# Layer 0's queries and keys projected by token instead of by feature, and the attention sink as a column of layer 1's scores

## Chip, core and metric

The kernel runs on one core of a Trainium2 chip. The metric is the device time of one execution in microseconds (us), lower is better; several runs are timed and their median counts. The engines are TensorE (PE; its weight loads are PEld), VectorE (DVE), ScalarE (ACT), GpSimd (POOL) and SyncE (SP), which here issues nearly all transfers.

## What is computed

A decoder trunk with two layers over 256 tokens of width 1024, all in float32. Layer 0 is causal attention over 16 heads of 64 (with 256 tokens its blocks of 256 leave plain causal attention), layer 1 is sliding-window attention (window 128) of 16 query heads over 4 shared key/value heads with a learned sink per head. Each layer ends in a gated FFN (width 2816) with a causal depthwise convolution of width 3. In each head the first 16 of 64 dimensions of queries and keys are rotated.

```python
def partial_rope(x, cos, sin):
    x1, x2 = x[..., :half], x[..., half:ROT_DIM]           # half = 8
    return concat([x1 * cos - x2 * sin, x2 * cos + x1 * sin, x[..., ROT_DIM:]])

# layer 0
h = rmsnorm(x, attn_norm[0])
q, k, v = split(h @ w_qkv_a[0], 3)
q, k = partial_rope(heads(q)), partial_rope(heads(k))
o = causal_attention(q, k, heads(v))
# layer 1
logits = where(band, q @ k.T / 8, NEG)
m = maximum(max(logits), sink)
e = exp(logits - m)
p = e / (sum(e) + exp(sink - m))
# both layers
x = x + o @ w_o
x = x + conv_ffn(rmsnorm(x, ffn_norm[l]), ...)
```

## The kernel before

**Precision and weights.** Every matmul is done in three: each operand is split into a high part (rounded to the fast float32 format of TensorE) and a low part, and high x high, high x low and low x high are added in PSUM. Weights come in 90 units of 128 x 2048 numbers (1 MB each, tile `wr`, three buffers). For each unit ScalarE makes the high part `wh` (`hi_part`, L173) and VectorE the low part `wl` (`lo_part`, L181), in two to eight pieces, four buffers each. Unit i + 3 is fetched when unit i has been split, and unit i + 4 is split when the matmuls of unit i have been issued. Units 2 to 7 and 10 to 11 are layer 0's query and key weights (two for each group of four heads), 0, 1, 8 and 9 its value weights, 12 to 15 its output weights.

**Order.** All engines' queues are filled by one Python program. It keeps a clock of estimated TensorE time (`tick`); work on other engines is put off with `chain(key, (delay, step), ...)` and issued when that clock has passed its time, or earlier when `require(key)` asks for it. So the delays in the code set the order in each engine's queue, and the queues are executed strictly in that order.

**Layer 0's queries and keys** (`qk_group`, `proj_f`, `rotate_f`). Weights are the stationary operand and the normalized activations the moving one (256 tokens), so the product has features on partitions and tokens in columns: one PSUM bank (`acc`, 128 x 512) holds two chunks of 128 features of q, another of k. Rotation in that layout: VectorE swaps neighbours within 32 partitions (`stream_shuffle`, L460), multiplies the bank and the swapped copy by two tables (L461, L462) and adds (L463); ScalarE makes the high part (L466), VectorE the low part (L471). The tables `tab` have cosines and sines by feature and token, already multiplied by the token's 1/rms; `new_tables` scales them by token on ScalarE (L433) and turns them with four transposes on TensorE (L440). Group 0 is projected with its q and k banks in turn, groups 1 to 3 one bank after the other.

**Layer 1's queries and keys** (`proj`, `rotate`, `rope`, `to_feature`) already go by token: activations stationary, weights moving, the product scaled by 1/rms as ScalarE copies it out of PSUM (L1098), rotated on VectorE in four small operations on the 16 rotated dimensions (L391, L396 twice, L397), transposed by TensorE (L403), split into high (ScalarE, L414) and low part (VectorE, L409).

**Attention.** For each of four groups: `scores` (18 matmuls), for each head a mask and a running minimum on VectorE (`masked`, L548), exponentials with their sum on ScalarE (`exps`, L558), reciprocal and scaling (`norm`, VectorE L569 and L576, ScalarE L574), transposes of the probabilities on TensorE (`probs_T`, L589) with copies out of PSUM (L595, L597), and `values` (L612). Between these, `fill` puts matmuls of a filler: projections of the next groups and of the other half of v (L362 to L364), then the output projection (L662 to L667). `spread` copies the first token block of k into a block-diagonal tile `kd` on GpSimd (L1002), which the scores of the first token block need. Of PSUM there are four banks `acc`, two `u` and two `t`.

**The sink** in layer 1: the minimum of negated scores starts at -sink (`nsink`), a ScalarE exponential gives exp(sink - m) for each head (L561), and VectorE adds it to the sum (L567).

Of the kernel before, what the change touches and what calls it, by code (L numbers as in the profile page):

```python
# [7 lines left out]
F32 = mybir.dt.float32  # L8
# [52 lines left out]
def trunk(ctx: ExitStack, tc, x, xw, pos, cpk, fin, sinks, w, out):  # L61
# [26 lines left out]
    def row3(n=3 * P):  # L88
        return wk.tile([P, 3 * P], F32, tag="m3", name=nm("m3"), bufs=8)[:, :n]
# [308 lines left out]

    def to_feature(t, n, b, hi, lo, key, then=None):

        pt = bank("t")
        for j in range(n):
            nc.tensor.transpose(pt[:, j * P:(j + 1) * P], t[:, j * P:(j + 1) * P], ident)  # L403
        tick(110 * n)
        v = pt[:, :n * P].rearrange("p (j t) -> p j t", j=n)
        hb, lb = hi[:, :, blk(b)], lo[:, :, blk(b)]

        def low():
            nc.vector.tensor_tensor(out=lb, in0=v, in1=f(hb), op=ALU.subtract)  # L409
# [12 lines left out]

    tab = [None]
    TURN = 7700.0

    def new_tables(rs_, key, between):

        ex = tab[0]
        sc = mid().rearrange("p (b k f) -> p b k f", b=NB, k=2)
        new = quad(F32, "tab")[:, :2]  # L430

        for b in range(NB):
            nc.scalar.activation(sc[:, b], ex[:, b].rearrange("p k e d -> p k (e d)"), AF.Copy, scale=rs_[b])  # L433
            between(b)

        def turn():
            t = bank("t")
            for b in range(NB):
                for k in range(2):
                    nc.tensor.transpose(t[:, k * S + b * P:k * S + (b + 1) * P], sc[:, b, k], ident)  # L440
            tick(440)
            chain(key, (300.0, lambda: copy(t)))

        def copy(t):
            nc.scalar.activation(new, t.rearrange("p (k t) -> p k t", k=2), AF.Copy)
            tab[0] = new

        chain(key, (TURN, turn))

    SWAP = [(i + HALF) % ROT if i < ROT else i for i in range(32)]  # L450

    def rotate_f(o, hi, lo, key, tkey, then=None):

        t, u = mid(), mid()
        t3, u3, o3 = (a.rearrange("p (c t) -> p c t", c=2) for a in (t, u, o))

        def turn():
            require(*tkey)
            c_, s_ = (tab[0][:, k].unsqueeze(1).to_broadcast([P, 2, S]) for k in range(2))
            nc.vector.stream_shuffle(u, o, SWAP)  # L460
            nc.vector.tensor_tensor(out=t3, in0=o3, in1=c_, op=ALU.mult)  # L461
            nc.vector.tensor_tensor(out=u3, in0=u3, in1=s_, op=ALU.mult)  # L462
            nc.vector.tensor_tensor(out=t, in0=t, in1=u, op=ALU.add)  # L463

        def high():
            nc.scalar.activation(hi, t3, AF.Copy)  # L466
            if then is not None:
                then(hi, 0)

        def low():  # L470
            nc.vector.tensor_tensor(out=lo, in0=t3, in1=f(hi), op=ALU.subtract)  # L471
            if then is not None:
                then(lo, 1)

        chain(key, (150.0, turn), (2600.0, high), (700.0, low))

    def proj_f(o, hT, wv, units=()):

        for m in range(2):
            om = o[:, m * S:(m + 1) * S]  # L480
            for c in range(KC):
                for b in range(NB):
                    require("x", b, c // 4)
                xh, xl = hx(hT, c)
                wh, wl = wv(c, m)
                nc.tensor.matmul(om, wh, xh, start=(c == 0), stop=False)
                nc.tensor.matmul(om, wh, xl, start=False, stop=False)
                nc.tensor.matmul(om, wl, xh, start=False, stop=(c == KC - 1))
                tick(3 * S / 2.4)
                if m and units and (c + 1) * len(units) % KC == 0:  # L490
                    used(units[(c + 1) * len(units) // KC - 1])
                yield 3 * S / 2.4

    def cols128(u, n_u, at):

        def wv(c, m):
            i, r = divmod(c * n_u, KC)
            need(u + i)
            w_ = UNIT * n_u // KC
            s_ = slice(r // n_u * w_ + at + m * P, r // n_u * w_ + at + (m + 1) * P)  # L500
            return tuple(t[:, s_] for t in wq[u + i])
        return wv

    def attention(qk, ready, filler, lead, rate, msk, vcol, sink):
# [35 lines left out]
        def softmax(j, p, sd, sab):  # L540
            pr = [row3() for _ in range(2)]
# [11 lines left out]
            def exps(e):  # L553
                h = 2 * j + e
                c2 = slice(2 * e, 2 * e + 2)
                for qb in range(NB):
                    c = slice(P, 3 * P) if qb else slice(0, P)
                    nc.scalar.activation(pr[e][:, c], pr[e][:, c], AF.Exp, scale=-1.0, bias=st[:, 0, 2 * e + qb:2 * e + qb + 1],  # L558
                                         accum_out=st[:, 1, 2 * e + qb:2 * e + qb + 1])
                if sink:  # L560
                    nc.scalar.activation(st[:, 2, c2], st[:, 0, c2], AF.Exp, bias=sink_t[:, h:h + 1])  # L561

            def norm(e):
                c2 = slice(2 * e, 2 * e + 2)
                total = st[:, 1, c2]
                if sink:
                    nc.vector.tensor_tensor(out=st[:, 2, c2], in0=total, in1=st[:, 2, c2], op=ALU.add)  # L567
                    total = st[:, 2, c2]
                nc.vector.reciprocal(st[:, 3, c2], total)  # L569
                for qb in range(NB):  # L570
                    c = slice(P, 3 * P) if qb else slice(0, P)
                    r = st[:, 3, 2 * e + qb:2 * e + qb + 1]
                    if qb:
                        nc.scalar.activation(pr[e][:, c], pr[e][:, c], AF.Copy, scale=r)  # L574
                    else:
                        nc.vector.tensor_scalar(out=pr[e][:, c], in0=pr[e][:, c], scalar1=r, scalar2=None, op0=ALU.mult)  # L576
# [371 lines left out]
    def tables():  # L948
        nc.vector.scalar_tensor_tensor(out=kk, in0=arg[:, 0], scalar=-1.0, in1=arg[:, 0], op0=ALU.mult, op1=ALU.max)
        nc.gpsimd.tensor_scalar(out=arg[:, 1], in0=kk, scalar1=-1.0, scalar2=HALF_PI, op0=ALU.mult, op1=ALU.add)  # L950
# [6 lines left out]
        ex = mid().rearrange("p (b k e d) -> p b k e d", b=NB, k=2, e=2)  # L957
        nc.gpsimd.memset(ex[:, :, 0, :, ROT:], 1.0)
        nc.gpsimd.memset(ex[:, :, 1, :, ROT:], 0.0)
        for k, t in enumerate((cs, sn)):  # L960
            for e in range(2):
                nc.gpsimd.tensor_copy(ex[:, :, k, e, :ROT], t)
        tab[0] = ex
# [48 lines left out]
    nc.gpsimd.tensor_scalar(out=nsink, in0=sink_t, scalar1=-1.0, scalar2=0.0, op0=ALU.mult, op1=ALU.add)  # L1012
# [43 lines left out]
    attention(qk, ready_a, filler_a(), 9000.0, lambda g: (7000.0, 3500.0, 2000.0) if g < 3 else (4500.0, 2000.0, 1500.0), mask, lambda h: h, False)  # L1056
# [12 lines left out]
    o_down[0].finish(3, after_a, by_half=True)  # L1069
    xT_h = new_hT()  # L1070
# [114 lines left out]
def pack(inp):  # L1185
# [14 lines left out]
    qk = [np.concatenate([q[:, :, g * 256:(g + 1) * 256], k[:, :, g * 256:(g + 1) * 256]], axis=2) for g in range(4)]  # L1200
# [72 lines left out]
```

## Time and profile before

| | |
|---|---|
| median of 3 runs | 558.45 us (557.94 to 558.82) |
| profiled execution | 559.24 us, span 557.2 us |
| granted TensorE clock | 0.999 |
| busy, share of span | PE 97%, PEld 91%, DVE 78%, ACT 68%, POOL 21% |
| HBM read | 99.30 MB, mean 180 GB/s |
| layer 0's attention | 16 to 118 us; layer 1's: 295 to 371 us |

The span is the time from the first to the last instruction of the profiled execution; the rest of its time lies around it. Busy time of TensorE counts matmuls whose ends are modelled and which overlap, so the distances between starts tell more than the shares. A group of instructions is told as line, engine, operation, out<-in, shapes, count, then busy us and mean ns of one, then the idle time before it and what ended it.

### The profile page before, as it was taken

The numbers are of one execution on the slowest core, as the hardware profiler recorded it, in microseconds if no ns is written. First come the engines' busy times: TensorE is split into PE (matmuls) and PEld (weight loads), VectorE is DVE, ScalarE is ACT, GpSimd is POOL, SyncE is SP. The second block draws the span as 40 slices with busy tenths as digits, with TensorE's granted clock in tenths as the row PEclk, the third lists the DMA queues.
The fourth block names the chain that finished last, engine by engine and source line by source line (L and its number), as shares of the span: only waits on it lengthen the run. The fifth ranks groups of instructions, "written<-read, shape, count | busy, mean of one in ns | idle before, by whom it ended". The sixth has DMA issues, their size and how long they took to land.

```text
span 557.2 us, 10523 instructions
## 1 busy us (share of the span) xinstructions
PE 543.3 (97%) x4022; PEld 507.3 (91%) x4022; DVE 435.8 (78%) x930; ACT 376.7 (68%) x765; POOL 115.1 (21%) x130
## 2 busy tenths in 40 slices
PE   9998999999999999999999999999999999999995
PEld 8997789889999999988888988889999999998884
DVE  6799888599888888873468988888888888884514
ACT  6749697779567777654358998887757777663313
POOL 8322202012333322210001000001632322210003
PEclk9999999999999999999999999999999999999999
DMA  8954462523365656666552724242375556666301
GB/s 326 372 204 168 155 228 92 212 80 149 131 248 205 199 207 223 226 227 203 184 216 89 289 78 151 76 145 85 123 256 191 203 213 226 233 228 215 118 0 75
DMA packets 15312, 101.00 MB, mean 181 GB/s; under 512 B 1952, under 2 KB 2080, under 8 KB 3744
## 3 DMA queue, kind: packets, MB, share of 16 engines
q1 hardware_dynamic: 14976, 100.09, 50.3%
q8 instruction: 31, 0.51, 0.4%
q10 hardware_dynamic: 288, 0.26, 0.1%
q14 instruction: 17, 0.14, 0.1%
HBM read 99.30 MB, written 1.05 MB: 180 GB/s over the span
## 4 chain that ended last, share of the span: by engine, by line
PE 76%; DVE 10%; ACT 5%; DMA 5%; issue 2%; POOL 0%; SPq 0%; DVEq 0%; POOLq 0%; ACTq 0%
PE acc L662 9%; PE acc L663 9%; PE acc L667 9%; PE u L758 6%; PE u L757 6%; PE u L759 6%; PE t L758 6%; PE t L757 6%; PE t L759 6%; DMA wr<-in_w 4%; DVE wl L181 3%; PE acc L757 2%; PE acc L759 2%; PE acc L758 2%; PE t L612 2%
## 5 line engine op out<-in xcount | busy, mean ns | idle before, releaser
L181 DVE TENSOR_TENSOR wl<-wr,wh 128x1024 fp32r<-128x1024 f32 (+1 forms) x190 | 208.1, 1111 | 49.5 <-ACT wh L173 49.2
L173 ACT ACTIVATE wh<-wr 128x1024 fp32r<-128x1024 f32 (+1 forms) x186 | 174.4, 964 | 52.0 <-PE acc L667 42.3
L803 POOL TENSOR_TENSOR m<-m,m 128x256 f32<-128x256 f32 x44 | 72.7, 1653 | 164.8 <-DVE m L798 99.3
L662 PE MATMUL acc<-wh,q 128*128 128x512 f32 x238 | 92.1, 387 | 0.0
L663 PE MATMUL acc<-wl,q 128*128 128x512 f32 x238 | 90.6, 380 | 0.0
L757 PE MATMUL u<-q,wh 128*128 128x256 f32 x320 | 88.3, 277 | 0.0
L758 PE MATMUL u<-q,wh 128*128 128x256 f32 x320 | 88.1, 276 | 0.0
L759 PE MATMUL u<-q,wl 128*128 128x256 f32 x320 | 87.9, 275 | 0.0
L757 PE MATMUL t<-q,wh 128*128 128x256 f32 x288 | 79.2, 275 | 0.0
L758 PE MATMUL t<-q,wh 128*128 128x256 f32 x288 | 79.2, 275 | 0.0
L759 PE MATMUL t<-q,wl 128*128 128x256 f32 x288 | 79.2, 275 | 0.0
L667 PE MATMUL acc<-wh,q 128*128 128x512 f32 x238 | 74.6, 379 | 0.0
L759 PEld LDWEIGHTS u<-q,wl 128*128 128x128 f32 x320 | 61.4, 192 | 0.0
L758 PEld LDWEIGHTS u<-q,wh 128*128 128x128 f32 x320 | 61.4, 192 | 0.0
L757 PEld LDWEIGHTS u<-q,wh 128*128 128x128 f32 x320 | 61.3, 192 | 0.0
L757 PEld LDWEIGHTS t<-q,wh 128*128 128x128 f32 x288 | 55.3, 192 | 0.0
L758 PEld LDWEIGHTS t<-q,wh 128*128 128x128 f32 x288 | 55.3, 192 | 0.0
L759 PEld LDWEIGHTS t<-q,wl 128*128 128x128 f32 x288 | 55.3, 192 | 0.0
L662 PEld LDWEIGHTS acc<-wh,q 128*128 128x128 f32 x238 | 45.0, 189 | 7.0 <-issue 0.7
L667 PEld LDWEIGHTS acc<-wh,q 128*128 128x128 f32 x238 | 45.0, 189 | 6.3
L663 PEld LDWEIGHTS acc<-wl,q 128*128 128x128 f32 x238 | 45.0, 189 | 5.9 <-issue 0.2
L807 ACT ACTIVATE q<-m 128x256 fp32r<-128x256 f32 x44 | 18.2, 416 | 45.4 <-POOL m L803 45.3
(191 smaller groups left out, 1152.6 us busy)
## 6 DMA issues: line engine op xcount, KB each, us to landing
wr<-in_w SPq DMA_DIRECT2D x90, 1024.0 KB, 4.8
first<-in_xw SPq DMA_DIRECT2D x5, 384.0 KB, 5.2
xr<-in_x SPq DMA_DIRECT2D x2, 512.0 KB, 8.4
first<-in_xw SPq DMA_DIRECT2D x1, 768.0 KB, 6.6
fin_t<-in_fin SPq DMA_DIRECT2D x1, 512.0 KB, 5.6
out<-ot SPq DMA_DIRECT2D x1, 512.0 KB, 2.6
first<-in_xw SPq DMA_DIRECT2D x1, 388.0 KB, 3.3
out<-m ACTq DMA_DIRECT2D x1, 256.0 KB, 2.1
```

Source lines behind the costliest of these rows:

```text
L173: nc.scalar.activation(wq[i][0][:, c], raws[i][:, c], AF.Copy, **({} if g is None else {"scale": g}))
L181: nc.vector.tensor_tensor(out=wq[i][1][:, c], in0=raws[i][:, c], in1=f(wq[i][0][:, c]), op=ALU.subtract)
L612: nc.tensor.matmul(o[:, P:] if kb else o, v_sb[kb][:, vcol(2 * j + e)], pT[p][e][:, S:] if kb else pT[p][e][:, :S], start=(kb == 0), stop= ...
L662: nc.tensor.matmul(pairs(o), ph[:, blk(b)], turns(hi[:, s_]), start=first, stop=False)
L663: nc.tensor.matmul(pairs(o), ph[:, blk(b)], turns(lo[:, s_]), start=False, stop=False)
L667: nc.tensor.matmul(pairs(o), pl[:, blk(b)], turns(hi[:, s_]), start=False, stop=end)
L757: nc.tensor.matmul(pairs(o), hi[:, s_], xh, start=(c == 0), stop=False)
L758: nc.tensor.matmul(pairs(o), hi[:, s_], xl, start=False, stop=False)
L759: nc.tensor.matmul(pairs(o), lo[:, s_], xh, start=False, stop=(c == KC - 1))
L803: nc.gpsimd.tensor_tensor(out=h, in0=gs, in1=t[1], op=ALU.mult)
L807: (3400.0, lambda: nc.scalar.activation(hi, h, AF.Copy)),
```

## The change

Layer 0's queries and keys go by token as layer 1's do: `qk_group` uses `proj` with 512 columns of q and k of a group as moving operand (the weights' columns are stored turned, in `pack`), two token blocks b, one bank `acc` each; `qk_out` scales by 1/rms; `rotate` then rotates, transposes (four transposes for each block) and splits. `proj_f`, `cols128`, `rotate_f` and `new_tables` go, with the tables' expansion. Groups 0 and 1 are projected with their two blocks in turn (`TOGETHER`). The delay from rotation to transposes becomes 1300 for layer 1 too (`TRANS`), the high part has its own step, the time that filler runs before the first scores goes from 9000 to 8000. Unit 4 is split with two of its four high parts on ScalarE. In layer 1 each row of scores gets a column for the sink beside it (before the first block's 128 columns, behind the second block's 256); GpSimd copies -sink there, the exponentials and their sum run over 129 and 257 columns, and the separate exponential and addition go. The rows' tiles are 8 columns longer in both layers and in the FFN.

```diff
     def row3(n=3 * P):
-        return wk.tile([P, 3 * P], F32, tag="m3", name=nm("m3"), bufs=8)[:, :n]
+        return wk.tile([P, 3 * P + 8], F32, tag="m3", name=nm("m3"), bufs=8)[:, 4:4 + n]
+
+    def sink_row():
+        t = wk.tile([P, 3 * P + 8], F32, tag="m3", name=nm("m3"), bufs=8)
+        return t[:, 4:4 + 3 * P], (t[:, 3:4 + P], t[:, 4 + P:5 + 3 * P])
...
+    TRANS = 1300.0
+
     def to_feature(t, n, b, hi, lo, key, then=None):
...
+        def high():
+            nc.scalar.activation(hb, v, AF.Copy)
+            if then is not None:
+                then(hi, 0)
+
         def low():
             nc.vector.tensor_tensor(out=lb, in0=v, in1=f(hb), op=ALU.subtract)
             if then is not None:
-                then(hi, 0)
                 then(lo, 1)
 
-        chain(key, (200.0, lambda: nc.scalar.activation(hb, v, AF.Copy)), (600.0, low))
+        chain(key, (200.0, high), (600.0, low))
...
-              (1000.0, lambda: to_feature(t, n, b, hi, lo, key, then)))
+              (TRANS, lambda: to_feature(t, n, b, hi, lo, key, then)))
...
         def softmax(j, p, sd, sab):
-            pr = [row3() for _ in range(2)]
+            pr, with_sink = zip(*(sink_row() for _ in range(2)))
+            if sink:
+                for e in range(2):
+                    h = 2 * j + e
+                    for t in (with_sink[e][0][:, :1], with_sink[e][1][:, S:]):
+                        nc.gpsimd.tensor_copy(t, nsink[:, h:h + 1])
...
             def exps(e):
...
-                    c = slice(P, 3 * P) if qb else slice(0, P)
-                    nc.scalar.activation(pr[e][:, c], pr[e][:, c], AF.Exp, scale=-1.0, bias=st[:, 0, 2 * e + qb:2 * e + qb + 1],
+                    c = with_sink[e][qb] if sink else pr[e][:, P:] if qb else pr[e][:, :P]
+                    nc.scalar.activation(c, c, AF.Exp, scale=-1.0, bias=st[:, 0, 2 * e + qb:2 * e + qb + 1],
                                          accum_out=st[:, 1, 2 * e + qb:2 * e + qb + 1])
-                if sink:
-                    nc.scalar.activation(st[:, 2, c2], st[:, 0, c2], AF.Exp, bias=sink_t[:, h:h + 1])
...
-    new_tables(rs, ("rt",), lambda b: (v_out(b, 0, v_acc[b]), both_parts(4, 2 + b)))
+    both_parts(4, 1)
+    rs.append(rstd_of(1))
+    for k in range(2, 4):
+        part(4, quarter(k))
     fetch(7)
+    for b in range(NB):
+        v_out(b, 0, v_acc[b])
...
+    TOGETHER, WAIT = 2, 1500.0
+
+    def qk_out(t, b, o):
+        nc.scalar.activation(t, o, AF.Copy, scale=rs[b])
 
     def qk_group(g, u):
         hi, lo = quad(), quad()
-        o = [bank("acc") for _ in range(2)]
-
-        def finish(n):
-            c = slice(2 - 2 * n, 4 - 2 * n)
-            rotate_f(o[n], hi[:, c], lo[:, c], ("qk", g), ("rt",), None if n else lambda src, w: spread(g, src, w))
-
-        gens = [proj_f(o[n], hT, cols128(u, 2, S - n * S), (u, u + 1) if n else ()) for n in range(2)]
-        if g == 0:
+        o = [bank("acc") for _ in range(NB)]
+
+        def finish(b):
+            rotate(o[b], 4, b, hi, lo, ("qk", g), lambda t: qk_out(t, b, o[b]),
+                   None if b else lambda src, w: spread(g, src[:, 2:4], w), WAIT)
+
+        gens = [proj(o[b], hT, b, cols512(u), (u, u + 1) if b else ()) for b in range(NB)]
+        if g < TOGETHER:
             for _ in range(KC):
                 yield sum(next(gen) for gen in gens)
-        for n in range(2):
-            yield from gens[n]
-            finish(n)
+        for b in range(NB):
+            yield from gens[b]
+            finish(b)
...
-    attention(qk, ready_a, filler_a(), 9000.0, ...
+    attention(qk, ready_a, filler_a(), 8000.0, ...
```

On VectorE, between the low parts of unit 5 and the first scores of layer 0, there stood two rotations of a whole bank (a bank is `acc`, the rotated copy `m`):

```order
L460 STREAM_SHUFFLE m_26_420<-acc_345 128x512
L461 TENSOR_TENSOR m_25_419<-acc_345,tab_315 128x512
L462 TENSOR_TENSOR m_26_420<-m_26_420,tab_315 128x512
L463 TENSOR_TENSOR m_25_419<-m_25_419,m_26_420 128x512
L460 STREAM_SHUFFLE m_29_456<-acc_346 128x512
L461 TENSOR_TENSOR m_28_455<-acc_346,tab_315 128x512
L462 TENSOR_TENSOR m_29_456<-m_29_456,tab_315 128x512
L463 TENSOR_TENSOR m_28_455<-m_28_455,m_29_456 128x512
L471 TENSOR_TENSOR q_344<-m_25_419,q_343 128x512
L181 TENSOR_TENSOR wl_481<-wr_279,wh_480 128x1024
L471 TENSOR_TENSOR q_344<-m_28_455,q_343 128x512
```

In that place VectorE has now (the lines of the changed kernel: L397 to L403 are `rope`, L422 the low part out of the transposes' bank `t`):

```order
L397 TENSOR_TENSOR rb<-m_22_383,cs 128x128
L402 TENSOR_TENSOR rb<-m_22_383,sn 128x8x8 x2
L403 TENSOR_TENSOR m_22_383<-rb 128x8x16
L397 TENSOR_TENSOR rb<-m_23_384,cs 128x128
L402 TENSOR_TENSOR rb<-m_23_384,sn 128x8x8 x2
L403 TENSOR_TENSOR m_23_384<-rb 128x8x16
L187 TENSOR_TENSOR wl_401<-wr_272,wh_400 128x1024
L422 TENSOR_TENSOR q_332<-t_424,q_331 128x4x128
L187 TENSOR_TENSOR wl_401<-wr_272,wh_400 128x1024
L422 TENSOR_TENSOR q_332<-t_429,q_331 128x4x128
L187 TENSOR_TENSOR wl_446<-wr_311,wh_445 128x1024 x2
```

Four operations on 512 columns became four on 128 and 64, and both low parts of unit 7 (`wl_446`) follow at once, ahead of the first mask.

On ScalarE, after the exponentials of group 0 in layer 0, these stand behind the last matmul of group 2's first block in the changed kernel (L502 scales probabilities, L179 makes high parts of weights, L417 high parts of q and k, L523 copies transposed probabilities, L949 is `qk_out` for that block):

```order
L179 ACTIVATE wh_570<-wr_452 128x1024
L502 ACTIVATE m_37_506<-m_37_506,hst_507 128x256
L179 ACTIVATE wh_570<-wr_452 128x1024
L417 ACTIVATE q_385<-t_589 128x4x128
L417 ACTIVATE q_385<-t_594 128x4x128
L523 ACTIVATE m_48_614<-u_610 128x384
L949 ACTIVATE m_51_625<-acc_526,rstd_297 128x512
```

Its transposes on TensorE follow on those of the last two probability rows, ahead of the matmuls of the second block:

```order
L517 MATMUL u_652<-ident,m_36_505 128x128 x3
L517 MATMUL u_657<-ident,m_37_506 128x128 x3
L411 MATMUL t_662<-ident,m_51_625 128x128 x4
L368 MATMUL acc_527<-wh_445,q_107 128x512
L369 MATMUL acc_527<-wl_446,q_107 128x512
```

So a TensorE queue in which the rotation had no place now has a step that needs ScalarE's copy and VectorE's rotation.

On ScalarE in layer 1, the first exponentials of group 0 before:

```order
L558 ACTIVATE m_342_3914,hst_3916<-m_342_3914,hst_3916 128x128
L558 ACTIVATE m_342_3914,hst_3916<-m_342_3914,hst_3916 128x256
L561 ACTIVATE hst_3916<-hst_3916,sink_t 128x2
L558 ACTIVATE m_343_3915,hst_3916<-m_343_3915,hst_3916 128x128
L558 ACTIVATE m_343_3915,hst_3916<-m_343_3915,hst_3916 128x256
L561 ACTIVATE hst_3916<-hst_3916,sink_t 128x2
```

and now:

```order
L492 ACTIVATE m_338_3746,hst_3752<-m_338_3746,hst_3752 128x129
L492 ACTIVATE m_338_3746,hst_3752<-m_338_3746,hst_3752 128x257
L492 ACTIVATE m_339_3747,hst_3752<-m_339_3747,hst_3752 128x129
L492 ACTIVATE m_339_3747,hst_3752<-m_339_3747,hst_3752 128x257
L502 ACTIVATE m_338_3746<-m_338_3746,hst_3752 128x256
```

The small exponentials are gone and the others are one column wider.

More of the change, by code (lines that the diff above doesn't have):

```diff
@@ L420, in rotate @@
               (wait, lambda: rope(t.rearrange("p (h d) -> p h d", d=HD), 2 * n, b)),
-              (1000.0, lambda: to_feature(t, n, b, hi, lo, key, then)))
[L423 to L502, printed above, removed]
+              (TRANS, lambda: to_feature(t, n, b, hi, lo, key, then)))
     def attention(qk, ready, filler, lead, rate, msk, vcol, sink):
@@ L553, in exps @@
             def exps(e):
-                h = 2 * j + e
-                c2 = slice(2 * e, 2 * e + 2)
                 for qb in range(NB):
-                    c = slice(P, 3 * P) if qb else slice(0, P)
-                    nc.scalar.activation(pr[e][:, c], pr[e][:, c], AF.Exp, scale=-1.0, bias=st[:, 0, 2 * e + qb:2 * e + qb + 1],
+                    c = with_sink[e][qb] if sink else pr[e][:, P:] if qb else pr[e][:, :P]
+                    nc.scalar.activation(c, c, AF.Exp, scale=-1.0, bias=st[:, 0, 2 * e + qb:2 * e + qb + 1],
                                          accum_out=st[:, 1, 2 * e + qb:2 * e + qb + 1])
-                if sink:
-                    nc.scalar.activation(st[:, 2, c2], st[:, 0, c2], AF.Exp, bias=sink_t[:, h:h + 1])
             def norm(e):
                 c2 = slice(2 * e, 2 * e + 2)
[L565 to L569, printed above, removed]
+                nc.vector.reciprocal(st[:, 3, c2], st[:, 1, c2])
                 for qb in range(NB):
@@ L948, in tables @@
     def tables():
-        nc.vector.scalar_tensor_tensor(out=kk, in0=arg[:, 0], scalar=-1.0, in1=arg[:, 0], op0=ALU.mult, op1=ALU.max)
-        nc.gpsimd.tensor_scalar(out=arg[:, 1], in0=kk, scalar1=-1.0, scalar2=HALF_PI, op0=ALU.mult, op1=ALU.add)
         nc.scalar.activation(trig, arg, AF.Sin)
@@ L956, in tables @@
                                     op0=ALU.mult)
[L957 to L963, printed above, removed]
+    nc.vector.scalar_tensor_tensor(out=kk, in0=arg[:, 0], scalar=-1.0, in1=arg[:, 0], op0=ALU.mult, op1=ALU.max)
+    nc.gpsimd.tensor_scalar(out=arg[:, 1], in0=kk, scalar1=-1.0, scalar2=HALF_PI, op0=ALU.mult, op1=ALU.add)
     for j in range(4):
@@ L988, in trunk @@
             square(b, n)
-        both_parts(4, b)
-        rs.append(rstd_of(b))
-    new_tables(rs, ("rt",), lambda b: (v_out(b, 0, v_acc[b]), both_parts(4, 2 + b)))
+    both_parts(4, 0)
+    rs.append(rstd_of(0))
+    both_parts(4, 1)
+    rs.append(rstd_of(1))
+    for k in range(2, 4):
+        part(4, quarter(k))
     fetch(7)
+    for b in range(NB):
+        v_out(b, 0, v_acc[b])
     for k in range(4):
@@ L1011, in trunk @@
     nsink = one.tile([P, NH], F32, name="nsink")
-    nc.gpsimd.tensor_scalar(out=nsink, in0=sink_t, scalar1=-1.0, scalar2=0.0, op0=ALU.mult, op1=ALU.add)
     def v_half(n, u):
@@ L1054, in ready_a @@
         o_down.append(Down(U_OA, 4, oT, lambda i: require("o", i)))
-    attention(qk, ready_a, filler_a(), 9000.0, lambda g: (7000.0, 3500.0, 2000.0) if g < 3 else (4500.0, 2000.0, 1500.0), mask, lambda h: h, False)
+    attention(qk, ready_a, filler_a(), 8000.0, lambda g: (7000.0, 3500.0, 2000.0) if g < 3 else (4500.0, 2000.0, 1500.0), mask, lambda h: h, False)
     nc.gpsimd.affine_select(out=mask[:, :P], in_=mask[:, :P], compare_op=ALU.is_gt, fill=NEG, base=0,
@@ L1069, in trunk @@
     o_down[0].finish(3, after_a, by_half=True)
+    nc.gpsimd.tensor_scalar(out=nsink, in0=sink_t, scalar1=-1.0, scalar2=0.0, op0=ALU.mult, op1=ALU.add)
     xT_h = new_hT()
@@ L1199, in pack @@
     q, k, v = (m[:, :, i * D:(i + 1) * D] for i in range(3))
-    qk = [np.concatenate([q[:, :, g * 256:(g + 1) * 256], k[:, :, g * 256:(g + 1) * 256]], axis=2) for g in range(4)]
+    qk = [turned(np.concatenate([q[:, :, g * 256:(g + 1) * 256], k[:, :, g * 256:(g + 1) * 256]], axis=2)) for g in range(4)]
     v = turned(v)
```

## Prediction

> **What bounds the kernel now.** I read the waits of the TensorE first, then its order of time around each wait, then busy time by stage, then the groups for prices. The span is 557.2 us and TensorE is busy in 97% of it, so only two things can move the end: how long its own instructions take, and the few places where it waits. The long waits (engine, line, releaser: us in total, times, longest):
>
> ```profile
> PE acc L488 <- DVE wl L181: 2.0, 1, 2.0
> PE u L589 <- DVE m L576: 1.3, 1, 1.3
> PE u L589 <- ACT m L595: 1.3, 1, 1.3
> ```
>
> The first two fall into layer 0's attention, the third into layer 1's. Busy time by stretch (PE, PEld, DVE, ACT, POOL) says who is short there:
>
> ```profile
> 40.00:55.00 15.00, 12.74 (x107) 11.92 (x104) 14.97 (x42) 12.66 (x30) 3.98 (x4) 1.00 0.53 187
> 55.00:70.00 15.00, 13.65 (x91) 11.53 (x89) 13.35 (x36) 10.47 (x27) 3.28 (x4) 1.00 0.43 156
> 316.00:332.00 16.00, 14.62 (x134) 13.65 (x132) 13.49 (x57) 13.77 (x37) 0.00 (x0) 1.00 0.44 160
> ```
>
> From 40 to 55 us VectorE is busy for 14.97 of 15.00 us, ScalarE for 12.66: VectorE makes TensorE wait. The same places in order of time (start, duration):
>
> ```profile
> 24.81 0.38 PE L440 MATMUL t<-ident,m 128*128 128x128 f32 x2
> 25.97 0.36 PE L486 MATMUL acc<-q,wh 128*128 128x256 f32 x1
> ...
> 43.37 0.28 PE L487 MATMUL acc<-q,wh 128*128 128x256 f32 x1
> 45.67 0.38 PE L488 MATMUL acc<-q,wl 128*128 128x256 f32 x1 [2.03 <-DVE wl L181]
> ...
> 49.82 0.33 PE L589 MATMUL u<-ident,m 128*128 128x128 f32 x1
> 50.57 0.37 PE L486 MATMUL acc<-q,wh 128*128 128x256 f32 x1
> ...
> 68.15 0.38 PE L364 MATMUL acc<-wh,q 128*128 128x512 f32 x1
> 69.87 1.27 PE L589 MATMUL u<-ident,m 128*128 128x128 f32 x6 [1.35 <-DVE m L576]
> 70.90 0.46 PE L362 MATMUL acc<-wh,q 128*128 128x512 f32 x1
> ...
> 326.08 0.49 PE L589 MATMUL u<-ident,m 128*128 128x128 f32 x3
> 327.82 0.55 PE L589 MATMUL u<-ident,m 128*128 128x128 f32 x3 [1.25 <-ACT m L595]
> 328.12 0.36 PE L362 MATMUL acc<-wh,q 128*128 128x256 f32 x1
> ```
>
> Durations overlap on TensorE, so its cost is the distance between starts. The next rows give that for 256 columns (33 distances), for 512 (35 distances of six matmuls) and for four transposes:
>
> ```profile
> 16.26 0.28 PE L488 MATMUL acc<-q,wl 128*128 128x256 f32 x1
> 20.01 0.28 PE L488 MATMUL acc<-q,wl 128*128 128x256 f32 x1
> 237.95 0.43 PE acc L667 x2
> 283.28 0.43 PE acc L667 x2
> 114.25 0.60 PE L290 MATMUL t<-ident,xr 128*128 128x128 f32 x4
> 114.61 0.46 PE L662 MATMUL acc<-wh,q 128*128 128x512 f32 x1
> ```
>
> That is 3.75 / 33 = 0.1136 us, 45.33 / 210 = 0.2159 us, and 0.36 us for a set of four.
>
> **The change, part by part.** (1) Projection: 384 matmuls of 256 columns become 192 of 512: 192 x 0.2159 - 384 x 0.1136 = 41.5 - 43.6 = **-2.2 us** on TensorE, all on the path.
>
> (2) Eight sets of four transposes (four groups, two token blocks) come in: 8 x 0.36 = **+2.9 us**. The Trainium skill, "TensorE: Matmul & The Clock Gate", Part 4, gives about 275 ns for one transpose in a kernel; four would cost 1.1 us and the eight sets 8.8. By that rule the trace disagrees: its L290 lasts near that long, but the next matmul starts 0.36 us after the first of four.
>
> (3) The table transposes (L440) go: from 24.81 to 25.97, **-1.2 us**, waiting for the scaled tables included.
>
> (4) VectorE. Now one bank costs four full-width operations and a difference; the prices:
>
> ```profile
> 29.27 0.74 DVE L460 STREAM_SHUFFLE m<-acc 128x512 f32<-128x512 f32 x1
> 31.83 0.74 DVE L460 STREAM_SHUFFLE m<-acc 128x512 f32<-128x512 f32 x1
> ...
> 43.06 2.56 DVE L181 TENSOR_TENSOR wl<-wr,wh 128x1024 fp32r<-128x1024 f32 x2
> ```
>
> ```profile
> L471 DVE TENSOR_TENSOR q<-m,q 128x512 fp32r<-128x512 f32 x8 | 5.7, 711 | 2.4 <-ACT q L466 2.4
> L391 DVE TENSOR_TENSOR rb<-m,cs 128x64 f32<-128x64 f32 x10 | 2.2, 222 | 0.9 <-ACT m L1098 0.7
> L396 DVE TENSOR_TENSOR rb<-m,sn 128x32 f32<-128x32 f32 x20 | 3.0, 187 | 0.0
> L876 ACT ACTIVATE v<-acc,rstd 128x512 f32<-128x512 f32 x4 | 2.7, 672 | 0.0
> L618 ACT ACTIVATE q<-t 128x512 fp32r<-128x512 f32 x8 | 4.7, 584 | 3.4 <-PE t L612 3.4
> L173 ACT ACTIVATE wh<-wr 128x1024 fp32r<-128x1024 f32 (+1 forms) x186 | 174.4, 964 | 52.0 <-PE acc L667 42.3 <-DMA wr<-in_w 2.9 <-PE t L758 2.8
> ```
>
> Before: 31.83 - 29.27 = 2.56 and 0.71, times 8: 26.2 us. After, the rope works on 128 and 64 columns: between 0.9 us (all at L391's 0.222) and 1.6 (L391 and L396 doubled); by the slope of the two rows (35 ns for 32 columns) 2 x 0.29 + 2 x 0.22 = 1.0. With the difference 1.7 x 8 = 13.9 us. VectorE is freed of 12 us where it was full. ScalarE gets 8 copies out of PSUM, 8 x 0.67 = 5.4 us; the high parts stay (0.58).
>
> So what did the waits hang on? At 43.37 on a weight's low part, which VectorE made in a pair (43.06, 2.56 us) behind a mask and a part of a later unit; now both parts of that unit stand ahead of the first mask. I take this wait as gone: 45.67 - 43.37 - 0.11 = -2.2. At 68.15 it was the last probabilities of group 1, behind VectorE's queue: -1.5 (69.87 - 68.15 - 0.22) and -0.5 inside the set (70.90 - 69.87 = 1.03; six at 0.09 are 0.54). At 49.82 three transposes took 0.75 for 0.27: -0.5. Together **-4.7 us**; the bounds are 0 (other work gets late in their place) and -6 (smaller gaps go too). I take the end near the upper, as 12 us of VectorE's work leave 65 us of stage.
>
> What is late next: group 2's first block. After its last matmul TensorE has twelve transposes of probabilities and fifteen matmuls, 2 x 0.54 + 15 x 0.216 = 4.3 us, and then the four transposes of that block, in whose way stand on ScalarE two weight halves, a scaling, two high parts, a row copy and the block's own copy.
>
> ```profile
> L574 ACT ACTIVATE m<-m,hst 128x256 f32<-128x256 f32 x32 | 14.4, 498 | 0.0
> L595 ACT ACTIVATE m<-u 128x384 f32<-128x384 f32 x24 | 10.7, 481 | 1.0 <-PE u L589 1.0
> 35.21 2.14 POOL L1002 CAST kd<-q 64x256 fp32r<-64x256 f32 x2 [1.21 <-DVE q L471]
> ```
>
> 2 x 0.96 + 0.50 + 2 x 0.58 + 0.48 + 0.67 + 1.0 (rope) = 5.7 us, less about 0.1 for each of six ScalarE starts that overlap: 5.1. TensorE waits for **+0.8 us** there, with everything behind it in its queue; bounds 0 and 1.4. The other sets have 18 or 21 matmuls of 512 ahead of them (3.9 us and more), or scores and values of about that length: nothing. First scores: GpSimd copies the diagonal keys, two pairs of up to 2.14 us, behind the first block's high part (0.58); 0.36 + 21 x 0.216 = 4.9 us of TensorE lie between that block's transposes and those scores, so they just cover 0.58 + 4.28 = 4.86. I take nothing; a VectorE that is late with the low part would cost some tenths.
>
> (5) The sink's column. ScalarE loses 16 small exponentials, VectorE 16 sums; GpSimd, at 0.00 busy us from 316 to 332, gets 64 single-column copies, which must land before the exponentials of rows that TensorE freed a group earlier.
>
> ```profile
> L561 ACT ACTIVATE hst<-hst,sink_t 128x2 f32<-128x2 f32 x16 | 4.6, 285 | 0.0
> L567 DVE TENSOR_TENSOR hst<-hst 128x2 f32<-128x2 f32 x16 | 2.3, 154 | 0.5 <-ACT hst L561 0.4
> 19.51 0.20 POOL L954 COPY cs<-rb 128x16 f32<-128x16 f32 x1
> ```
>
> At 0.20 us each, eight copies of a group are 1.6 us, beside a group's dozens of matmuls. The wait at 326.08 (328.12 - 326.08 = 2.04 for six transposes, 0.54 without it) hangs on ScalarE's row copy L595, which four L561 precede; they start about 0.2 us before their successors, so 0.8 us of 1.5 goes. Against that the transposes of q move three matmuls (0.34) closer to the first scores. I take **-0.7 us**, with 0 and -2.5 as bounds (all of that stage's gaps).
>
> Sum: -2.2 + 2.9 - 1.2 - 4.7 + 0.8 - 0.7 = **-5.1 us**. The profiled execution took 559.24 us (557.2 span and 2.0 around it), 0.8 above the median of 558.45. So 554.1 for that execution, **553.3 us** for the median. Everything behind layer 0 is bound by TensorE's own starts, so a gain there is not given back.
>
> **The rivals.** *The waits come back elsewhere.* Floor alone: -2.2 + 2.9 - 1.2 = -0.5, or 557.9 us. For it: ScalarE was at 12.66 of 15 and gets more. Against it: VectorE, named by three of the four waits, loses twice as much.
>
> *Slower: the chain copy, rope, transpose, high, low is longer than TensorE's cover.* A transpose is in TensorE's queue, and all behind it waits. The gain without any such wait is 5.9 us over eight sets, so the sign turns when each set waits for 0.74 us on average; at 1.5 us each it is 12 - 5.9 = +6, 564.5 us. For it: my walk finds 0.8 us at one set. Against: the other sets have 3.9 us of matmuls ahead.
>
> *Transposes at full length.* If starts do not overlap in the new place, each costs L290's duration, near 0.28 us: 8 x 4 x 0.28 = 9.0 instead of 2.9, and 559.4 us: no change to a little slower. This is also the Trainium skill's 275 ns, "TensorE: Matmul & The Clock Gate", Part 4. The row at 114.25 speaks against it.
>
> *More goes than I count.* All waits and small gaps of both attentions: -0.5 - 6 - 2.5 = -9.0, 549.5 us.
>
> **How the numbers follow.** Forecast 0.64, returning waits 0.13, the long chain 0.08, transposes at full length 0.03, more gained 0.12. Range 550.5 to 557.0: it leaves out the slower cases (0.11), most of the returning waits and the far end of the largest gain. A measurement tells about 0.2%, 1.1 us, from no change. Faster: 0.64 + 0.12 + 0.03 of the returning waits = 0.79; same 0.10 + 0.03 = 0.13; slower 0.08.
>
> **What would show it.** Right: no wait of TensorE for a low part near 43 us, VectorE well below full from 40 to 55, sets of four transposes at about 0.36 us, a wait below 1.5 us at the transposes of group 2, first scores of layer 0 about 2 us earlier, a shorter wait near 326. Wrong: waits of TensorE's transposes for VectorE's rope, exponentials that wait for GpSimd, or six matmuls of 512 columns that take more than 1.30 us in the projection.

## The result and the profile after

The changed kernel takes **554.36 us** (median of 4 runs, 553.85 to 555.22) against 558.63 us for the kernel before (4 runs, 557.94 to 559.09): 4.27 us less, a ratio of 0.9926 with a 95% interval of 0.9908 to 0.9944. Forecast were 553.3 us and a gain of 5.1. The profiled execution took 554.76 us, with a span of 553.0.

Where the time went is read from two marks in the order of time: the first up-projection matmul of each FFN. Rows of before, then of after (start, duration):

```profile
117.76 0.47 PE L757 MATMUL u<-q,wh 128*128 128x256 f32 x2
374.29 0.48 PE L757 MATMUL u<-q,wh 128*128 128x256 f32 x2
```

```profile
114.47 0.48 PE L685 MATMUL u<-q,wh 128*128 128x256 f32 x2
370.37 0.48 PE L685 MATMUL u<-q,wh 128*128 128x256 f32 x2
```

Up to the first mark, which is layer 0's attention, 3.29 us are gone (forecast 4.4). Between the marks, with layer 1's attention, it is 256.53 - 255.90 = 0.63 us (forecast 0.7). The rest, 0.3 us of span and 0.3 around it, lies behind the second mark and is no more than executions differ by.

TensorE's waits after (engine, line, releaser: us in total, times, longest):

```profile
PE u L278 <- DVE warm L254: 1.1, 1, 1.1
PE u L517 <- ACT m L523: 0.8, 1, 0.8
PE acc L368 <- ACT v L804: 0.7, 1, 0.7
PE t L411 <- ACT wh L179: 0.6, 1, 0.6
PE t L411 <- DVE m L403: 0.6, 1, 0.6
```

The waits for a low part (2.0 us) and for the probabilities (1.3) are gone. The first line, the start, was there before. The last three lie in layer 0, and only the last of them had been forecast. Their places in time:

```profile
26.78 0.38 PE L370 MATMUL acc<-wh,q 128*128 128x512 f32 x1
27.81 0.48 PE L368 MATMUL acc<-wh,q 128*128 128x512 f32 x1 [0.65 <-ACT v L804]
...
31.80 0.60 PE L411 MATMUL t<-ident,m 128*128 128x128 f32 x4
33.00 0.63 PE L411 MATMUL t<-ident,m 128*128 128x128 f32 x4 [0.60 <-ACT wh L179]
33.38 0.46 PE L368 MATMUL acc<-wh,q 128*128 128x512 f32 x1
...
38.00 0.28 PE L459 MATMUL acc<-kd,q 128*128 128x256 f32 x1
...
51.38 0.49 PE L517 MATMUL u<-ident,m 128*128 128x128 f32 x3
52.46 0.66 PE L411 MATMUL t<-ident,m 128*128 128x128 f32 x4 [0.60 <-DVE m L403]
52.87 0.46 PE L368 MATMUL acc<-wh,q 128*128 128x512 f32 x1
...
322.53 0.49 PE L517 MATMUL u<-ident,m 128*128 128x128 f32 x3
323.87 0.55 PE L517 MATMUL u<-ident,m 128*128 128x128 f32 x3 [0.85 <-ACT m L523]
```

Taking off each time the distance that there is without a wait, TensorE stands still for 0.82 us at 27, 0.82 at 32 and 0.81 at 52. The wait of layer 1 that stood at 326.08 before is now the one at 323.87, shorter by about 0.4 (1.25 to 0.85 in the brackets). The sets of four transposes take 0.38 and 0.41 us to the next matmul. The stages, in the columns of the prediction's table:

```profile
40.00:55.00 15.00, 14.40 (x79) 12.59 (x78) 12.97 (x43) 13.79 (x34) 2.70 (x5) 1.00 0.59 211
55.00:70.00 15.00, 15.00 (x96) 12.89 (x95) 10.36 (x36) 12.49 (x31) 1.63 (x4) 1.00 0.38 141
312.00:328.00 16.00, 15.15 (x139) 14.22 (x138) 13.33 (x51) 13.82 (x35) 2.11 (x8) 1.00 0.48 180
```

TensorE went from 12.74 to 14.40 us of 15 and from 13.65 to 15.00, VectorE from 14.97 to 12.97 and from 13.35 to 10.36; ScalarE took over more.

### The profile page after: what moved, and what is told of

It is laid out like the page before. It is cut to its first block, busy times and chain, and to the rows that moved or that the text cites. A ratio compares the mean times of both kernels' runs of the same rounds, so it can differ in the third digit from the quotient of the medians.

```text
span 553.0 us, 10213 instructions
## 1 busy us (share of the span) xinstructions
PE 542.7 (98%) x3858; PEld 501.7 (91%) x3858; DVE 420.7 (76%) x904; ACT 378.1 (68%) x756; POOL 116.6 (21%) x156
## 4 chain that ended last, share of the span: by engine, by line
PE 83%; DVE 6%; ACT 5%; DMA 3%; issue 1%; POOL 0%; SPq 0%; DVEq 0%; POOLq 0%; ACTq 0%
PE acc L590 9%; PE acc L595 9%; PE acc L591 9%; PE u L686 6%; PE u L685 6%; PE u L687 6%; PE t L686 6%; PE t L685 6%; PE t L687 6%; DVE wl L187 3%; PE acc L368 2%; PE acc L370 2%; PE acc L369 2%; DMA wr<-in_w 2%; PE acc L686 2%; PE acc L685 2%
## 5 line engine op out<-in xcount | busy, mean ns | idle before, releaser
L179 ACT ACTIVATE wh<-wr 128x1024 fp32r<-128x1024 f32 (+1 forms) x188 | 175.1, 960 | 50.6 <-PE acc L595 43.4
L731 POOL TENSOR_TENSOR m<-m,m 128x256 f32<-128x256 f32 x44 | 69.9, 1591 | 167.8 <-DVE m L726 87.9
L368 PE MATMUL acc<-wh,q 128*128 128x512 f32 (+1 forms) x160 | 56.0, 350 | 0.7 <-ACT v L804 0.7
L369 PE MATMUL acc<-wl,q 128*128 128x512 f32 (+1 forms) x160 | 54.1, 338 | 0.0
L370 PE MATMUL acc<-wh,q 128*128 128x512 f32 (+1 forms) x160 | 54.0, 337 | 0.0
L590 PEld LDWEIGHTS acc<-wh,q 128*128 128x128 f32 x238 | 45.0, 189 | 6.8 <-issue 0.7
```

The lines of the kernel that those rows point to most:

```text
L179: nc.scalar.activation(wq[i][0][:, c], raws[i][:, c], AF.Copy, **({} if g is None else {"scale": g}))
L368: nc.tensor.matmul(pairs(o), xh[:, blk(b)], turns(wh), start=(c == 0), stop=False)
L369: nc.tensor.matmul(pairs(o), xh[:, blk(b)], turns(wl), start=False, stop=False)
L370: nc.tensor.matmul(pairs(o), xl[:, blk(b)], turns(wh), start=False, stop=(c == KC - 1))
L590: nc.tensor.matmul(pairs(o), ph[:, blk(b)], turns(hi[:, s_]), start=first, stop=False)
L731: nc.gpsimd.tensor_tensor(out=h, in0=gs, in1=t[1], op=ALU.mult)
```

## The experiments

The theory: layer 0's gain is TensorE's waits for VectorE, the new form of TensorE's own work is worth almost nothing, and the sink's column carries 0.6 us. The rivals: the gain is in the form or order of TensorE's work; or the column carries more.

**The two halves of the change apart.** The changed kernel with the sinks as before:

```diff
-                    c = with_sink[e][qb] if sink else ...
+                    c = slice(P, 3 * P) if qb else slice(0, P)
...
+                if sink:
+                    nc.scalar.activation(st[:, 2, c2], st[:, 0, c2], AF.Exp, bias=sink_t[:, h:h + 1])
```

> The changed kernel with layer 1's sinks as they were before (an exp and an add of their own), layer 0 unchanged. Theory (layer 0 carries the gain, the sink column 0.6 us, by FFN starts 114.47 and 370.37 in the changed kernel's trace against 117.77 and 374.29 before): about 555.0 us, FFN of layer 0 starts at about 114.5, FFN of layer 1 at about 371.0. Rival (the sink column carries more than the milestones say, because a wait at 323 grows back behind ScalarE): 556 to 557.5 us.

And the kernel before with the column alone (the same lines the other way, and the rows with their two extra columns):

> The kernel before with the sink column alone. Theory: layer 0 unchanged, layer 1 shorter by about 0.6 us, so 557.9 us (faster by 0.1%). Rival (the column is worth all of ScalarE's 32 exps of about 0.2 us that it removes): 552 to 556 us. Rival (the exps lay beside other work): 558.5 us, no change.

Measured: 555.05 us (0.9929, 0.9912 to 0.9947) and 558.06 us (0.9990, 0.9976 to 1.0005). By the clock of whole runs 0.6 us can't be told from nothing; the marks can tell it. First with the old sinks, then with the column alone:

```profile
114.00 0.48 PE L688 MATMUL u<-q,wh 128*128 128x256 f32 x2
370.52 0.48 PE L688 MATMUL u<-q,wh 128*128 128x256 f32 x2
```

```profile
117.64 0.47 PE L760 MATMUL u<-q,wh 128*128 128x256 f32 x2
373.48 0.47 PE L760 MATMUL u<-q,wh 128*128 128x256 f32 x2
```

The stretch between the marks is 256.52 us with the old sinks, whatever layer 0 does (256.53 in the kernel before), and 255.84 with the column (255.90 in the changed kernel). So the column is worth 0.6 to 0.7 us in both kernels, and the two halves add up. The rivals that give it 1 us or more fall (the small exponentials that it removes are 16, not the 32 of the expectation above).

**VectorE's work taken away, in the old form.** If the waits come from VectorE, the kernel before must lose them when only VectorE has less to do:

```diff
             nc.vector.stream_shuffle(u, o, SWAP)
             nc.vector.tensor_tensor(out=t3, in0=o3, in1=c_, op=ALU.mult)
-            nc.vector.tensor_tensor(out=u3, in0=u3, in1=s_, op=ALU.mult)
-            nc.vector.tensor_tensor(out=t, in0=t, in1=u, op=ALU.add)
```

> The kernel before with two of VectorE's four operations of each rotation in layer 0 left out (the product with the sine table and the sum), about 1.3 us x 8 = 10 us off VectorE; TensorE's work, its order and ScalarE's unchanged; queries and keys are then only half rotated. Theory (the gain is VectorE's relief): TensorE's waits at 43.4, 49.8 and 68.2 shrink, 2 to 3.5 us faster, about 555.8 us. Rival (the gain is in the new form of TensorE's work, or the waits come from the split of weights alone): 558.5 us.

Measured: 555.25 us (554.34 to 556.30), ratio 0.9932 (0.9914 to 0.9949), 3.5 us less than the kernel before, run beside it (558.80), with TensorE's 256-column matmuls and table transposes all in place. So most of the gain comes without TensorE's new form, and the rival that puts it there falls. Its stages and its first mark:

```profile
40.00:55.00 15.00, 15.00 (x131) 14.73 (x130) 14.53 (x40) 14.16 (x34) 4.79 (x5) 1.00 0.51 167
55.00:70.00 15.00, 15.00 (x101) 13.07 (x100) 11.44 (x34) 13.17 (x32) 0.48 (x2) 1.00 0.59 201
112.94 0.47 PE L755 MATMUL u<-q,wh 128*128 128x256 f32 x2
```

TensorE waits nowhere from 40 to 70 us, and the mark moves by 117.76 - 112.94 = 4.82 us in this execution, which is one of the quicker ones of its kernel (554.35 us). VectorE is still busy for 14.53 of 15 us: what counted was not its share but that the low parts came in time.

**VectorE's work put back, in the new form.** Behind each rotation of layer 0 five more operations, then two, then eight:

```diff
         nc.vector.tensor_tensor(out=t[:, :, 0:ROT], in0=ta, in1=tb, op=ALU.add)
+        for _ in range(5 if nh == 8 else 0):
+            nc.vector.tensor_tensor(out=ta, in0=tb, in1=c, op=ALU.mult)
```

> The changed kernel with five more VectorE operations of 128x128 (about 0.28 us each, 1.4 us) behind each of layer 0's eight rotations: 11.2 us put back on VectorE, which is about what the change took off it; TensorE's own work unchanged; the five results are not used. Theory (the gain is TensorE's waits for the low parts that VectorE was late with): the waits come back, 2 to 3.5 us, so about 557 us, and the FFN of layer 0 starts at about 117. Rival (the gain is in the form and order of TensorE's own work): 554.4 us, within 0.5.

> The changed kernel with two more VectorE operations behind each of layer 0's rotations instead of five (about 0.56 us x 8 = 4.5 us). Theory of a threshold (VectorE has room in this stage, and waits come only when it is near full): 554.4 to 555.5 us. Rival (each us on VectorE costs the same part of a us, 4.6/11.2 = 0.41, as with five): 554.4 + 1.8 = 556.2 us.

> The changed kernel with eight more VectorE operations behind each of layer 0's rotations (about 2.24 us x 8 = 17.9 us). Theory of a threshold: beyond full, nearly each us more costs one, so 559.0 + 5 to 6.7 = 564 to 566 us. Rival (the same part of a us for each): 554.4 + 17.9 x 0.41 = 561.7 us.

Measured: two 554.50 us (0.9926, 0.9909 to 0.9942), five 559.00 us (1.0000, 0.9985 to 1.0014), eight 568.12 us (1.0172, 1.0156 to 1.0187). Five bring back the whole time of before though TensorE keeps its new form; they do so by waits at another place than before, so what this run shows is that time on VectorE counts in the new form too. Two cost 0.1 us by medians, and 0.34 us by the first mark between two traces in which unit 4 landed about equally early (114.34 with a first cast at 21.68, against 114.00 with the old sinks and 21.91). So there is slack, if not a whole one, and a fixed price per microsecond (1.8 us here) is wrong. TensorE's waits with five, then with eight:

```profile
PE t L413 <- DVE hst L499: 2.1, 1, 2.1
PE t L413 <- DVE m L403: 1.4, 2, 0.9
```

```profile
PE t L413 <- DVE m L403: 8.9, 3, 5.6
PE u L468 <- DVE q L424: 1.1, 1, 1.1
```

They stand at the transposes, behind VectorE's rope (the first row names a small reciprocal that VectorE runs beside it; rope's own last operation ends at 48.53 us in that trace and the transposes start at 48.68): this is the prediction's slower rival, which needs 1.4 us more per rotation (put behind it, and so ahead of what VectorE has next) to undo the gain. Five cost more than the 2 to 3.5 us expected, and eight more than one for one (9.1 us for 6.7 more on VectorE). A second trace with five was made for that:

> The kernel with five more VectorE operations again, for a second trace, since the first one (557.2 us) was the fastest of its runs and the median was 559.0. If the weights' landing sets the difference, this trace shows unit 4 landing at another time than 21.5 us and its waits longer in the same places (30 to 55 us); if not, the difference lies behind layer 0.

It took 558.44 us where the first trace was of 557.2, and its first mark lies at 118.19 us, 1.22 later than 116.97. The stages around the 2.1 us wait, in the first trace and in this one (the eighth column is TensorE's granted clock):

```profile
46.00:49.00 3.00, 0.94 (x7) 0.73 (x8) 2.90 (x16) 3.00 (x10) 0.00 (x0) 1.00 0.81 328
50.00:53.00 3.00, 3.00 (x18) 2.71 (x17) 3.00 (x4) 2.80 (x6) 1.84 (x2) 1.00 0.00 0
```

```profile
46.00:49.00 3.00, 0.87 (x6) 0.54 (x6) 2.90 (x16) 3.00 (x11) 0.00 (x0) 1.00 0.96 317
49.00:50.00 1.00, 1.00 (x7) 0.88 (x8) 0.93 (x5) 1.00 (x3) 0.00 (x0) 0.81 0.29 107
50.00:53.00 3.00, 3.00 (x12) 2.52 (x11) 2.97 (x5) 3.00 (x6) 1.66 (x2) 0.50 0.00 0
```

The wait is the same; behind it the clock is 1.00 in the one and 0.50 in the other for 3.4 us (0.38 of the us before 50, by its mean of 0.81, and the three behind it), with 12 matmuls begun instead of 18. The first cast of unit 4, whose landing I had suspected first, starts within 0.4 us (21.49 and 21.88). With eight operations both long waits come with such a stretch; the clock was 0.50 there from 37 to 39 and from 61 to 67 us:

```profile
36.00:37.00 1.00, 1.00 (x5) 0.81 (x4) 0.90 (x4) 0.90 (x2) 0.00 (x0) 0.75 0.00 0
37.00:39.00 2.00, 2.00 (x6) 1.62 (x5) 1.93 (x5) 2.00 (x3) 0.00 (x0) 0.50 0.01 4
39.00:40.00 1.00, 1.00 (x4) 0.77 (x4) 1.00 (x3) 1.00 (x2) 0.30 (x1) 0.54 0.00 0
...
62.00:66.00 4.00, 4.00 (x12) 3.37 (x13) 2.96 (x9) 0.60 (x1) 1.69 (x4) 0.50 0.55 231
66.00:67.00 1.00, 1.00 (x4) 0.82 (x3) 0.00 (x0) 0.05 (x1) 0.00 (x0) 0.50 0.00 0
```

From 36 to 40 that is 4 us less the full-speed work of 0.75 + 2 x 0.50 + 0.54, and from 62 to 67 it is 5 less 2.5: 1.7 + 2.5 = 4.2 us that no wait shows. How often it happened in the other runs no trace tells, but each run has its mean clock on record. One stretch of 3.4 us at half the clock takes 0.003 off it; the end of the program, where the clock also falls to 0.50 (from 549 us on in the changed kernel's trace), takes up to 0.004 in the traces. Of the twelve runs with five operations seven lie at 0.994 or 0.995, with a median of 559.18 us, and five at 0.997 or 0.998, with 557.63, which is 3.3 us above the changed kernel and within what was expected; of the kernel before, 19 of 43 lie at 0.995 or less; of the 38 runs of the versions without a wait of 2 us none lies below 0.996. So it seems common wherever such a wait stands, and with five it is the likely reason for a cost above 3.5 us, which is not shown run by run.

**The transposes doubled.**

```diff
-        for j in range(n):
-            nc.tensor.transpose(pt[:, j * P:(j + 1) * P], t[:, j * P:(j + 1) * P], ident)
+        for _ in range(2 if n == 4 else 1):
+            for j in range(n):
+                nc.tensor.transpose(pt[:, j * P:(j + 1) * P], t[:, j * P:(j + 1) * P], ident)
```

> The changed kernel with each of layer 0's eight sets of four transposes done twice into the same bank. Theory (a set costs 0.35 to 0.41 us of TensorE's time and nothing more): 8 x 0.36 = 2.9 us more, 557.3 us; 2.0 at least if two of the sets' waits swallow theirs. Rival (a transpose costs its full 275 ns, as the page on TensorE of the Trainium skill states): 8.8 us more, 563 us.

Measured: 556.27 us (0.9956, 0.9941 to 0.9972), 1.9 us more than the changed kernel and just under the least expected. All of layer 0's sets, from the first transpose to the next matmul, add up to 6.9 us for 64 transposes; in the changed kernel they are 3.2 us for 32 (without the wait at 33.00). So 32 more cost 3.7 us of TensorE, about 0.115 each. About half of that reaches the mark: its FFN starts at 115.92, 1.92 us later than with the old sinks, where unit 4 landed as early (first casts at 21.85 and 21.91 us); the rest went into waits of layer 0 that the old sinks' trace has (0.31, 0.62 and 0.90 us, at 32, 51 and 52) and this one has not. (Against the changed kernel's 114.47 it is 1.45 us, but there unit 4 landed at 23.23, and part of its waits are due to that.) The rival's full length for each falls: the row below has 273 ns for one transpose while the next begins after about 0.11, and 32 of 273 ns would have been 8.7 us.

```profile
L412 PE MATMUL t<-ident,m x64: 272/273/328, 31.1 to 91.2; 128*128 128x128 f32 x64
```

**The unforeseen waits.** What leads to the bank that TensorE waits for at 27.81, in the changed kernel:

```profile
23.23 0.43 DVE L902 CAST wh<-wr 128x512 fp32r<-128x512 f32 x1 [3.31 <-DMA wr<-in_w]
25.68 0.15 DVE L352 TENSOR_TENSOR st<-st 128x1 f32<-128x1 f32 x1
26.11 0.93 POOL L354 TENSOR_TENSOR rstd<-st,mhalf 128x1 f32<-128x1 f32 x1 [0.63 <-DVE st L353]
27.07 0.69 ACT L804 ACTIVATE v<-acc,rstd 128x512 f32<-128x512 f32 x1 [0.88 <-POOL rstd L354]
27.66 2.18 ACT L179 ACTIVATE wh<-wr 128x512 fp32r<-128x512 f32 x4
29.74 1.25 ACT L949 ACTIVATE m<-acc,rstd 128x512 f32<-128x512 f32 x2
```

The row factors stand on VectorE behind casts that wait for unit 4 (3.31 us), the values' copy waits for the second factor, and the split of unit 5 and group 0's copies follow on ScalarE. That order is not new. In the kernel before, too, the factors stand behind casts of unit 4; there the landing was earlier, and the values' copies follow it at about the same distance (2.69 and 4.00 us behind the first cast; 2.27 and 3.84 in the changed kernel):

```profile
21.63 0.43 DVE L981 CAST wh<-wr 128x512 fp32r<-128x512 f32 x1 [0.60 <-DMA wr<-in_w]
24.32 0.67 ACT L876 ACTIVATE v<-acc,rstd 128x512 f32<-128x512 f32 x1
25.63 0.67 ACT L876 ACTIVATE v<-acc,rstd 128x512 f32<-128x512 f32 x1
```

So the factors were put ahead:

```diff
+    for b in range(NB):
+        rs.append(rstd_of(b))
+    for b in range(NB):
+        v_out(b, 0, v_acc[b])
+        both_parts(4, b)
-    both_parts(4, 0)
-    rs.append(rstd_of(0))
...
```

> The changed kernel with the two row factors (sums, GpSimd power) and layer 0's first values written out ahead of the split of weight unit 4, not behind it. Theory (the two waits of 0.82 us at 26.8 and 33.0 come from the values' bank that is let go late, and from ScalarE's split of unit 5 standing behind it): both go, 554.4 - 1.6 = 552.8 us. Rival (unit 5's landing sets the end of that stretch, and the waits come back some us later): 554.4 us.

and then group 2's first transposes six matmuls back as well (2100 for 1300 in their step of the chain):

> As the kernel with the row factors first, and besides group 2's first block has its four transposes behind six more 512-column matmuls of TensorE's queue. Theory: the wait of 0.81 us at 52.5 goes too, 552.0 us. Rival (group 2's scores then wait for the later high and low parts): 552.8 us or more.

Measured: 553.26 us (552.99 to 553.42; 0.9896, 0.9879 to 0.9913) and **552.55 us** (552.34 to 552.92; 0.9884, 0.9868 to 0.9899), which is 6.2 us under the kernel before and 1.8 under the change. Of TensorE's waits the second kernel keeps the first two lines of the changed kernel's list, the start and one in layer 1. The waits at 27 and 32 went together with the first step, the forecast one at 52 with the second; nothing came back later. The first step gave 1.1 us by medians and 1.72 by the FFN's mark (112.75), with unit 4 as late (23.20 us); the second gave 0.7 us by medians and 0.46 by the mark (112.29).

**What moves the old form's runs.** Two second traces:

> The kernel before with half of the rotation left out, once more: its six runs lay at 554.3 to 554.7 and at 555.8 to 556.3 us, and the trace is of the lower kind. If this execution is of the upper kind and the first weights' landing makes the difference, TensorE shows waits in the first 45 us that the first trace did not have, and the FFN of layer 0 starts about 1.5 us later than 113.0; if the clock does, a stretch of some us at a granted clock below 1.00.

> The kernel before itself, for a second trace: its runs reach from 557.2 to 560.8 us. Expected: the same waits at 43, 50 and 68 us, the FFN of layer 0 at 117.8 within 1 us; what differs from the first trace lies in the waits for the first weights (20 to 30 us) or in a stretch at a lower granted clock behind the wait at 43.

The relieved old kernel took 556.23 us this time (554.35 in its first trace). Its weight unit 4 landed at 23.56 us, where it was 21.96, and its FFN began at 114.53:

```profile
23.56 0.43 DVE L979 CAST wh<-wr 128x512 fp32r<-128x512 f32 x1 [2.04 <-DMA wr<-in_w]
26.39 0.44 PE L440 MATMUL t<-ident,m 128*128 128x128 f32 x2 [0.95 <-ACT m L433]
```

1.60 us of landing became 1.59 us at the mark, through the first projection and the table transposes. The kernel before took 558.73 us; its wait at 43 is the same (2.2 us), behind it the clock fell, and the waits at 50 and 68 are missing. I read that as a slower TensorE that gave VectorE time to catch up, which is argued and not shown. The mark lies at 117.2. The trace with the column alone, which has the same layer 0, speaks for it at a full clock: its unit 4 landed at 23.04 us, its first scores came 1.4 us later than before (39.70 for 38.33), the wait at 43 is 2.1 us, that at 68 is missing, and the mark is at 117.64.

```profile
48.00:49.00 1.00, 1.00 (x6) 1.00 (x6) 1.00 (x4) 1.00 (x2) 0.00 (x0) 0.50 0.95 401
```

## Why the prediction was right

**TensorE's own work** (-2.2 + 2.9 - 1.2 = -0.5 forecast). The two kernels without waits in layer 0 but for the tables, the relieved old one (112.94) and the last version (112.29), are 0.65 us apart, so this holds in an execution in which unit 4 lands early. In one in which it lands late the relieved old kernel loses 1.6 us more. The sets of transposes were sized 0.3 us too low (3.2 for 2.9).

**The waits that go** (-4.7 forecast). Taking VectorE's work alone moved the mark by 4.82 us in the first trace and by 3.23 in the second, 3.5 by medians. So the sum of 4.7 fits the first pair of traces, and is about 1.2 us too large for the median. The mechanism, TensorE waiting for VectorE, is shown by the relief in the old form. The load does not put the old waits back; it shows that in the new form VectorE's lateness comes out at the transposes behind the rope.

**The wait at group 2's first block** (+0.8 forecast) came as 0.81 us in the row; moving the transposes took 0.7 us off the median and 0.46 off the mark.

**The step that failed** is "the other sets: nothing", and with it the part of term 3 that took TensorE's wait for the scaled tables as gone for good. That wait hung on the row factors, which VectorE makes behind its casts of unit 4. Without the tables TensorE meets the same factors at the values' bank and at group 0's copies, and when unit 4 lands late, it waits there: 0.82 us for the bank, and 0.82 us for the second rotation of group 0. So the first scores came at 38.00 and not 2 us earlier than the 38.33 of before; with the factors first they come at 36.29.

Much of this is the execution. In the trace with the old sinks, which has the same layer 0, unit 4's first cast starts at 21.91 and not at 23.23, the wait at 27 is missing, that at 32 is 0.31 us, another of 0.62 stands at 51, the first scores come at 36.69 (1.64 us earlier than before), and the mark is at 114.00. There the miss in layer 0 is 0.6 us, where it is 4.4 - 3.3 = 1.1 in the first trace. By the marks of the traces that account closes: 4.82 (relief) and 0.65 (the new form, 112.94 to 112.29) less 1.72 (what the factors first give back) and 0.46 (group 2's transposes) is 3.29; forecast were 4.7 and 0.5 less 0 and 0.8. The first scores before, and with the factors first:

```profile
38.33 0.29 PE L528 MATMUL acc<-kd,q 128*128 128x256 f32 x1
```

```profile
36.29 0.28 PE L459 MATMUL acc<-kd,q 128*128 128x256 f32 x1
```

**The sink's column** (-0.7 forecast) gave 0.63 to 0.69, but not as the sum has it: of the wait at 326.08 it took 0.4 us where 0.8 were forecast. The rest lies in smaller waits of layer 1 (with the old sinks the list has 0.4 us behind scalings on ScalarE and 0.3 behind VectorE there, for the changed kernel neither), and the moved transposes cost nothing to be seen (256.52 and 256.53 us between the marks). So the size came right partly by luck. The count of its copies was wrong: 32, not 64, and none was waited for.

```profile
L477 POOL COPY m<-nsink x32: 180/185/1212, 239.9 to 349.6; 128x1 f32<-128x1 f32 x32
```

## What to carry to other kernels

An engine that is full for one stage is worth relieving just up to the point at which its results come in time: 4.5 us of the 12 freed here could have been put back for 0.1 to 0.3 us, 11.2 could not. When a step is taken out of a hand-written order, look at what it waited for: here the wait of the tables for the row factors did not go with the tables, but came back at the next place that needs them, until the factors themselves were put earlier. One trace of each kernel is not enough for such small terms, since the landing of one transfer moved a mark by up to 1.6 us. A gain too small for the runs can be read between two marks of TensorE's order, if the stretch between them is otherwise the same (256.52 and 256.53, 255.84 and 255.90 us here).

## What the runs showed of the hardware

A wait of TensorE of some 2 us can cost more than itself: in one of the two traces with five operations, and in one of the two traces of the kernel before, the granted clock fell to 0.50 for 3.4 us behind it; in the others, and in the trace with the column alone, it stayed at 1.00. The Trainium skill, "TensorE: Matmul & The Clock Gate", Part 1, has the clock at one half after an idle window of about 3.4 us and at full speed again after a busy one of that length, in windows that run freely. The halving and its length agree; the idle time that sufficed here is shorter (2.1 us in the row of waits), and that the same wait does it in one execution and not in the next fits a free-running window, though no run here shows the window itself.

The same transfer, weight unit 4, landed at times that differ by 2 us from execution to execution (its first cast starts between 21.6 and 23.6 us in the traces in which that cast waits for it). The relieved old kernel, whose TensorE waits for what hangs on it, hands that on, 1.6 us for 1.6 us; the kernel before does not, since its later waits for VectorE take it up (marks at 117.64 and 117.76 us for landings at 23.04 and 21.63); the two versions with the factors first took it at 23.2 and 23.4 without a wait, and their five runs each lie within 0.6 us.
